# Sample states in more buffers, loads on the sync queue, and a different split of the down projection's hidden tiles

## The chip, the core and the metric

The kernel runs on one core of one Trainium2 chip. A core has TensorE (matmuls; its weight loads are listed apart as PEld), VectorE (DVE), ScalarE (ACT), GpSimd (POOL) and SyncE (SP). In this kernel SP and POOL compute almost nothing; they issue the DMA transfers, each in the order of its own instruction stream. An engine's instructions run in order, so an instruction that waits holds back everything behind it on that engine, and the same is true of a DMA issue on SP or POOL.

The metric is the device time of one execution in microseconds (us). Times are read from a profiled execution and from unprofiled repeats.

## The reference, cut to what matters

One step of a two-layer decoder on 1072 rows: 32 sample rows (8 sequences of 4), 16 meta rows and 1024 prompt rows, all of width 1024. Layer 0 mixes with two gated linear scans, layer 1 with a Mamba-2 scan. Each mixer is followed by a feed-forward network (FFN) with 2816 hidden columns, that is 22 hidden tiles of 128:

```python
def swiglu(x, w_gate, w_up, w_down):
    return (jax.nn.silu(x @ w_gate) * (x @ w_up)) @ w_down
...
    for l in range(DEPTH):
        hn = rmsnorm(x, norm_mix_pre[l])
        ...
        x = x + rmsnorm(mix.astype(x.dtype), norm_mix_post[l])
        ff = swiglu(rmsnorm(x, norm_ffn_pre[l]), ffn_w_gate[l], ffn_w_up[l], ffn_w_down[l])
        x = x + rmsnorm(ff.astype(x.dtype), norm_ffn_post[l])
```

Beside y, the step returns the new recurrent states. For the sample group a state is read, decayed, added to and written back: in layer 0 six blocks of 128 x 1024 numbers, in layer 1 32 blocks of 128 x 512.

## The kernel before

**Storage and precision.** A matrix product is made of three matmuls on split operands, high x high, low x high and high x low (`mm3`, L232 to L234). On-chip storage is 29 strips of 1072 columns, which `strip` hands out and `drop` gives back, first in, first out, beside the fixed tiles `xh` and `xl` (8 x 1072 columns each), two raw weight buffers (`raw`) and ten short-lived tiles of up to 384 columns (`tmp`, name `t`).

**Weights.** `Weights` loads raw tiles on SP (L71) into the two raw buffers, and turns them into what TensorE takes: plain units (`wh` by ACT, L129; `wl` by DVE, L130) of two strips each, or forms for a seven-product (Strassen-Winograd) 2 x 2 block scheme (sums by DVE, L97; high by ACT, L115; low by DVE, L116), a strip for four tiles, half a strip for fewer. A raw buffer is free when its last form is made. `pump(RING)` runs after each form that TensorE has used and makes forms until `RING` = 6 are ahead, or strips run out.

**An FFN, stage by stage.** (1) The first `PLAIN` = 3 hidden tiles of gate and up are plain products. (2) `quad_gu` makes hidden tiles 3 to 21, one call each: seven forms of 24 matmuls of 268 columns (the 1072 rows in four quarters of `Q` = 268; two time halves `tb`). DVE and ACT take the sums out of six PSUM banks (L419, L464, L473, L478); the next forms accumulate in the same banks, so a late DVE holds TensorE back. Hidden tiles are paired, and `store` splits seven combinations of a pair into high and low (L248 on ACT, L249 on DVE) and writes them to DRAM on POOL (L408, L409). The last hidden tile, 21, has no partner and is `alone`: `spill` splits it and writes it on SP (L633, L634). (3) `quad_down` multiplies the pairs by the down weights in five blocks of `DOWN` = (2, 2, 2, 2, 1) pairs: four output pairs p x seven forms x 2 x n x 3 matmuls of 268 columns, each form taken out of PSUM by DVE or ACT (L501, L503). The pieces of a block are fetched back from DRAM while the block before runs: some go into `xh` and `xl`, the others into strips `fo`. After each p of the last block, three adds (L514) put in the part that the halves share. (4) `kblock` multiplies the plain tiles, four of them (0, 1, 2 and 21), by their down weights: 3 column blocks b of 304, 384 and 384 columns, 8 output tiles, added to the result by DVE (L534). After each b, `side` queues the norm of that b (`postnorm` L301 to L315 and, in layer 0, the next `prenorm` L288 to L299). The next layer's first products need them (`D.need(("xn", b))`). In layer 1 the order of the b is 1, 2, 0.

**Side work.** `Driver` steps a queue of generators beside the main one: `RATE` steps for each step (one form) of the main work. During `quad_gu` of layer 0 it runs `even_samples` (rate 0.3): one strip `st`, loaded on SP (L1057), updated by DVE, written back on SP (L1073); the next load waits for that. During `quad_gu` of layer 1 it runs `odd_samples` (rate 0.55): one strip `ssm` with two states of 512 columns; `load` (L1542, on POOL) fetches state i + 1 into the buffer that state i - 1 has just been written from (L1560, on POOL). The write waits for DVE (L1558, L1559), and the load for the write to land. Both share POOL's order with the pairs' stores.

**Order.** The program's order is not quite the order on an engine: matmuls of one stage can stand among those of the stage before where their operands are ready.

Of the kernel before, what the change touches and what calls it, by code (L numbers as in the profile page):

```python
# [8 lines left out]
F32 = mybir.dt.float32  # L9
F32R = mybir.dt.float32r  # L10
# [7 lines left out]
KD = 8  # L18
# [10 lines left out]
Q = 268  # L29
# [133 lines left out]
class Core:  # L163
# [247 lines left out]
    def quad_gu(self, W, i, hook=None):  # L411


        nc = self.nc
# [5 lines left out]
        pair, odd = divmod(i - PLAIN, 2)  # L420
        alone = i == 21

# [5 lines left out]
        def second(ps, tb):  # L428

            if alone:  # L430
                self.spill(PLAIN, (2 * tb + 1) * Q, Q, gated(self.tmp(Q), ps, part(keep, 2, tb), tb))
            elif not odd:
                gated(part(hraw, 0, tb), ps, part(keep, 2, tb), tb)
            else:
                b22 = gated(self.tmp(Q), ps, part(keep, 2, tb), tb)
                t1 = part(hraw, 2, tb)
                t3 = self.tmp(Q)
                add(t3, b22, part(hraw, 0, tb), ALU.subtract)
                add(t1, b22, t1, ALU.subtract)
                self.store(pair, "s4", tb, b22)  # L440
                self.store(pair, "s3", tb, t3)
                self.store(pair, "s2", tb, t1)

        def first(ps, tb):
            hd = gated(self.tmp(Q), ps, part(keep, 0, tb), tb)
            if alone:
                self.spill(PLAIN, 2 * tb * Q, Q, hd)
            elif not odd:
                t1 = part(hraw, 2, tb)
                add(t1, part(hraw, 0, tb), hd, ALU.subtract)  # L450
                self.store(pair, "a11", tb, hd)
                self.store(pair, "s1", tb, t1)
            else:
                t4 = self.tmp(Q)
                add(t4, hd, part(hraw, 2, tb), ALU.subtract)
                self.store(pair, "a12", tb, hd)
                self.store(pair, "a22", tb, t4)
# [57 lines left out]

    def kblock(self, units, rows, acc, b, first):

        nc = self.nc
        c0, n = BLKS[b]
        for m0 in range(0, KD, KBW):  # L520
            ms = range(m0, m0 + KBW)
            pss = [self.ps(n) for m in ms]
            for i, (hi, lo) in enumerate(units):
                for m, ps in zip(ms, pss):
                    s = slice(m * P, (m + 1) * P)
                    self.mm3(ps, (hi.t[:, s], lo.t[:, s]),
                             (self.xh[:, rows[i], c0:c0 + n], self.xl[:, rows[i], c0:c0 + n]),
                             i == 0, i == len(units) - 1)
            for m, ps in zip(ms, pss):
                a = acc[m].t[:, c0:c0 + n]  # L530
                if first:
                    nc.scalar.activation(out=a, in_=ps, func=AF.Copy)
                else:
                    nc.vector.tensor_tensor(out=a, in0=a, in1=ps, op=ALU.add)  # L534
                yield

    def ffn(self, W, side, order=(0, 1, 2)):
# [25 lines left out]
        end = len(DOWN) - 1  # L563
        rows = range(1 - end % 2, KD, 2)
        pieces = lambda c: [(f, j) for f in range(7) for j in range(DOWN[c])]

# [12 lines left out]
        def fetch_plain(i):  # L579
            for dst, src in ((self.xh, self.oh), (self.xl, self.ol)):  # L580
                nc.sync.dma_start(out=dst[:, rows[i]].bitcast(F32), in_=src[:, i])

# [22 lines left out]
        for c, n in enumerate(DOWN):  # L605
            todo = [(fetch, c + 1, *x) for x in pieces(c + 1)] if c < end else [(fetch_plain, i) for i in range(PLAIN + 1)]
# [10 lines left out]
            self.drop(*own[c])  # L617
        self.drop(self.sums, *ap1)
        dn = W.take(PLAIN + 1)
        for k, b in enumerate(order):  # L620
            yield from self.kblock(dn, rows, acc, b, False)
            side(b, acc)
            if k == 0:
                W.pump(2)
        for u in dn:
            self.drop(*u)
        W.pump(4)


    def spill(self, kt, c0, n, src):  # L630
        hi, lo = self.tmp(n, F32R), self.tmp(n, F32R)
        self.split(src, hi, lo)
        self.nc.sync.dma_start(out=self.oh[:, kt, c0:c0 + n], in_=hi.bitcast(F32))  # L633
        self.nc.sync.dma_start(out=self.ol[:, kt, c0:c0 + n], in_=lo.bitcast(F32))  # L634

# [408 lines left out]
    def even_samples(self, prs):  # L1044

        nc, I, O = self.nc, self.I, self.O
        vm = self.strip(F32R, "vm")
        st = self.strip(F32, "st")
        for pr in prs:
            st_in, st_out = ("gl_in", "gl_s") if pr.gla else ("hg_in", "hg_s")  # L1050
            ks, vs = self.kst(pr)
            for e in range(2):
# [3 lines left out]
                if e == 0 or not pr.gla:  # L1056
                    nc.sync.dma_start(out=st.t[:, :1024], in_=I[st_in][:, f])  # L1057
                nc.vector.tensor_tensor(out=vm.t[:96, :1024].rearrange("p (s d) -> p s d", s=8),
                                        in0=vs[:96, e * P:(e + 1) * P].bitcast(F32).unsqueeze(1).to_broadcast([96, 8, P]),
                                        in1=self.onehot.unsqueeze(2).to_broadcast([96, 8, P]), op=ALU.mult)  # L1060
                yield
                for half in range(2):
                    ba = self.ps(512)
# [8 lines left out]
                if e == 1 or not pr.gla:  # L1072
                    nc.sync.dma_start(out=O[st_out][:, f], in_=st.t[:, :1024])  # L1073
                yield
        self.drop(vm, st, *self.kvs)

# [453 lines left out]
    def odd_samples(self, grs):  # L1530

        nc, I, O = self.nc, self.I, self.O
        sp = self.strip(F32, "ssm")
        v8 = lambda a: a.rearrange("p (h d) -> p h d", h=8)
        steps = [(gr, s) for gr in grs for s in range(8)]
        state = lambda i: sp.t[:, (i % 2) * 512:(i % 2) * 512 + 512]
        masked = lambda i: self.bxs[2].t[:, 512 + (i % 4) * P:512 + (i % 4) * P + P]
        bu = [None] * len(steps)

        def load(i):  # L1540
            gr, s = steps[i]
            nc.gpsimd.dma_start(out=state(i), in_=I["ss_in"][:, s, 512 * gr.g:512 * gr.g + 512])  # L1542
            nc.vector.tensor_scalar(out=masked(i)[:96], in0=self.bst(gr.g)[0][:96].bitcast(F32),
                                    scalar1=self.onehot[:, s:s + 1], scalar2=None, op0=ALU.mult)
# [4 lines left out]

        load(0)  # L1550
        yield
        for i, (gr, s) in enumerate(steps):
            S0 = state(i)
            if i + 1 < len(steps):
                load(i + 1)
            product(i)
# [4 lines left out]
            yield  # L1561
        self.drop(sp, *self.bxs)

# [130 lines left out]
    def ffn_units(self, l):  # L1694
# [8 lines left out]
        return s + [d[i] for i in (*range(PLAIN), 21)]  # L1703

# [4 lines left out]
PLAIN = 3  # L1709
DOWN = (2, 2, 2, 2, 1)  # L1710
RING = 6
ODD0 = 6
# [213 lines left out]
```

## Time and profile before

| | us |
|---|---|
| median of 3 runs | 3037.62 |
| lowest, highest | 3033.34, 3039.83 |
| profiled execution, its own time | 3033.33 |
| span of the profiled execution | 3031.6 |
| `quad_gu` of layer 0, by first and last matmuls | 673.3 to 1095.2 |
| `quad_down` of layer 0, four blocks of two pairs | 1095.2 to 1262.7 |
| its block of one pair, then `kblock`, taken together | 1262.7 to 1340.2 |
| first products of layer 1 after it | 1340.2 to 1437.9 |
| `quad_gu` of layer 1 | 2296.2 to 2759.2 |
| `quad_down` of layer 1, four blocks of two pairs | 2759.2 to 2926.0 |
| its block of one pair, `kblock`, last norms | 2926.0 to 3031.6 |

Positions are us from the start of the span. TensorE is busy for 95% of the span, by pipelined matmuls whose durations overlap. So its idle time by stage, and the number of matmuls that a stage gets through in a us, say more than the busy share.

### The profile page before, as it was taken

The page shows a single profiled execution, that of the slowest core. Times are in us where ns is not written, and L with a number is a line of the kernel's source. Part 1 is how long each engine was busy: PE and PEld are TensorE (multiplying, and loading weights), DVE is VectorE, ACT ScalarE, POOL GpSimd, SP SyncE. Part 2 cuts the span into 40 slices and gives each one's busy share as a digit, 9 for nine tenths or more (in the row PEclk, how much of TensorE's full clock was granted, in tenths as well). Part 3 has the DMA queues.
Part 4 walks back from the last instruction along what each step waited for, and adds up shares of the span by engine and source line. Part 5 has one row for each costly group of instructions (what it writes and reads, how often), then busy time and mean ns, then how long its engine had stood idle before and what let it go on. Part 6 is the DMA issues. An engine that isn't in the chain of part 4 may idle for free.

```text
span 3031.6 us, 54611 instructions
## 1 busy us (share of the span) xinstructions
PE 2881.8 (95%) x20386; PEld 2754.1 (91%) x20386; DVE 2242.1 (74%) x4977; ACT 1407.2 (46%) x3195; POOL 318.2 (10%) x615
## 2 busy tenths in 40 slices
PE   7999999999999999988999999999999998899996
PEld 7998989999999999988898988989999998889986
DVE  7645645687878868888877777764588787776887
ACT  6533435553434442246667585744354333335223
POOL 0000000002333310000000000000002343431000
PEclk9999999999999999999999999999999999999998
DMA  4121226334554486442444344476333554549644
GB/s 142 43 63 39 79 69 205 98 100 136 163 160 133 154 324 225 154 148 78 120 122 138 110 138 131 130 229 214 106 131 128 171 169 152 168 136 335 233 140 129
DMA packets 242169, 442.78 MB, mean 146 GB/s; under 512 B 36176, under 2 KB 172272, under 8 KB 241904
## 3 DMA queue, kind: packets, MB, share of 16 engines
q1 hardware_dynamic: 212592, 353.33, 36.6%
q0 software_dynamic: 29312, 85.97, 8.4%
q8 instruction: 160, 2.62, 0.4%
q14 instruction: 105, 0.86, 0.1%
HBM read 295.12 MB, written 144.07 MB: 145 GB/s over the span
## 4 chain that ended last, share of the span: by engine, by line
PE 41%; issue 14%; DVE 8%; POOL 6%; DMA 5%; ACT 2%; POOLq 0%; SPq 0%; DVEq 0%; ACTq 0%
PE ps L232 8%; PE ps L233 8%; PE ps L234 8%; POOL fd L409 3%; POOL fd L408 3%; PE qb L233 2%; PE qb L232 2%; PE qb L234 2%; DMA cumb<-cum_d 2%; PE qa L232 1%; PE qe L232 1%; PE qe L234 1%; PE qe L233 1%; PE qa L233 1%; PE qa L234 1%
## 5 line engine op out<-in xcount | busy, mean ns | idle before, releaser
L232 PE MATMUL ps<-xh,wh 128*128 128x384 f32 (+1 forms) x2520 | 839.3, 334 | 19.3 <-ACT xh L248 7.3
L233 PE MATMUL ps<-xh,wl 128*128 128x384 f32 (+1 forms) x2520 | 829.0, 329 | 8.8 <-DVE wl L130 8.8
L234 PE MATMUL ps<-xl,wh 128*128 128x384 f32 (+1 forms) x2520 | 829.2, 330 | 0.0
L232 PEld LDWEIGHTS ps<-xh,wh 128*128 128x128 f32 x2520 | 477.5, 190 | 43.0 <-issue 12.4
L233 PEld LDWEIGHTS ps<-xh,wl 128*128 128x128 f32 x2520 | 478.1, 190 | 15.4 <-DVE wl L130 10.8
L234 PEld LDWEIGHTS ps<-xl,wh 128*128 128x128 f32 x2520 | 476.9, 189 | 4.3 <-issue 1.9
L115 ACT ACTIVATE w_s<-sums 128x512 fp32r<-128x512 f32 (+2 forms) x292 | 147.3, 514 | 278.7 <-DVE sums L97 216.1
L232 PE MATMUL qa<-xh,w_a 128*128 128x268 f32 x688 | 201.7, 293 | 15.3 <-ACT t L478 15.2
L248 ACT ACTIVATE t<-t 128x268 fp32r<-128x268 f32 (+2 forms) x230 | 101.3, 442 | 226.7 <-DVE t L419 122.6
L408 POOL DMA_DIRECT2D fd<-t x252 | 137.0, 543 | 647.5 <-ACT t L248 619.6
L130 DVE TENSOR_TENSOR wl<-raw,wh 128x1024 fp32r<-128x1024 f32 (+1 forms) x113 | 138.1, 1224 | 85.3 <-ACT wh L129 70.8
L233 PE MATMUL qa<-xh,w_a 128*128 128x268 f32 x688 | 199.5, 290 | 0.0
L234 PE MATMUL qa<-xl,w_a 128*128 128x268 f32 x672 | 194.3, 289 | 0.0
L232 PE MATMUL qb<-t,w_s 128*128 128x268 f32 x608 | 176.2, 290 | 15.0 <-DVE t L419 14.8
L115 ACT ACTIVATE w_a<-raw 128x512 fp32r<-128x512 f32 (+2 forms) x214 | 107.3, 516 | 154.4 <-PE qb L234 52.5
L233 PE MATMUL qb<-t,w_s 128*128 128x268 f32 x608 | 174.9, 288 | 0.0
L234 PE MATMUL qb<-t,w_s 128*128 128x268 f32 x608 | 174.7, 287 | 0.0
L129 ACT ACTIVATE wh<-raw 128x1024 fp32r<-128x1024 f32 (+1 forms) x113 | 119.5, 1057 | 109.6 <-DMA raw<-in_wd 29.0
L116 DVE TENSOR_TENSOR w_s<-sums,w_s 128x512 fp32r<-128x512 f32 (+2 forms) x292 | 157.4, 546 | 16.7 <-ACT w_s L115 11.3
L232 PEld LDWEIGHTS qa<-xh,w_a 128*128 128x128 f32 x688 | 132.4, 192 | 20.1 <-ACT t L478 19.2
L116 DVE TENSOR_TENSOR w_a<-raw,w_a 128x512 fp32r<-128x512 f32 (+2 forms) x214 | 116.6, 550 | 38.1 <-ACT w_a L115 27.3
L409 POOL DMA_DIRECT2D fd<-t x252 | 137.0, 543 | 25.2 <-DVE t L249 4.8
(401 smaller groups left out, 7425.4 us busy)
## 6 DMA issues: line engine op xcount, KB each, us to landing
fd<-t POOLq DMA_DIRECT2D x504, 134.0 KB, 3.7
fo<-fd SPq DMA_DIRECT2D x54, 536.0 KB, 4.9
raw<-in_wg SPq DMA_DIRECT2D x44, 512.0 KB, 4.3
raw<-in_wu SPq DMA_DIRECT2D x44, 512.0 KB, 5.2
xh<-fd SPq DMA_DIRECT2D x40, 536.0 KB, 6.6
raw<-in_wd SPq DMA_DIRECT2D x40, 512.0 KB, 4.4
xl<-fd SPq DMA_DIRECT2D x32, 536.0 KB, 7.5
cumb<-cum_d SPq DMA_DIRECT2D x32, 512.0 KB, 5.7
```

The lines of the kernel that those rows point to most:

```text
L115: nc.scalar.activation(out=tiled(hi), in_=src, func=AF.Copy)
L116: nc.vector.tensor_tensor(out=tiled(lo), in0=src, in1=tiled(hi).bitcast(F32), op=ALU.subtract)
L129: c.nc.scalar.activation(out=hi.t[:, :w], in_=r, func=AF.Copy)
L130: c.nc.vector.tensor_tensor(out=lo.t[:, :w], in0=r, in1=hi.t[:, :w].bitcast(F32), op=ALU.subtract)
L232: nc.tensor.matmul(out, lhsT=wh, rhs=xh, start=first, stop=False, **kw)
L233: nc.tensor.matmul(out, lhsT=wl, rhs=xh, start=False, stop=False, **kw)
L234: nc.tensor.matmul(out, lhsT=wh, rhs=xl, start=False, stop=last, **kw)
L248: self.nc.scalar.activation(out=hi, in_=src, func=AF.Copy)
L408: self.nc.gpsimd.dma_start(out=self.fd[:, i, FORMS.index(f), o:o + Q], in_=hi.bitcast(F32))
L409: self.nc.gpsimd.dma_start(out=self.fd[:, i, FORMS.index(f), 2 * Q + o:2 * Q + o + Q], in_=lo.bitcast(F32))
```

## The change

The diff does four things.

- `odd_samples` gets two strips, that is four states; `load` is issued on SP and three steps ahead; the mask that it used to make (L1543) becomes a step of its own, still one ahead. `even_samples` gets two strips `st`; the load of the next state is issued on SP one state ahead, and the write moves from SP to POOL.
- `RING` falls from 6 to 5.
- `DOWN` becomes (2, 2, 2, 2). `ALONE` = 19: hidden tiles 19, 20 and 21 have no partner, and `REST` lists the six plain tiles of the down projection: 0, 1, 2, 19, 20, 21. So `kblock` multiplies six tiles instead of four. The operands of the last two lie in four `fo` strips, the others in `xh` and `xl`.
- The `alone` tiles are written by `spill` on POOL instead of SP.

```diff
-        alone = i == 21
+        alone = i >= ALONE
...
-                self.spill(PLAIN, 2 * tb * Q, Q, hd)
+                self.spill(REST.index(i), 2 * tb * Q, Q, hd, nc.gpsimd)
...
         def fetch_plain(i):
-            for dst, src in ((self.xh, self.oh), (self.xl, self.ol)):
-                nc.sync.dma_start(out=dst[:, rows[i]].bitcast(F32), in_=src[:, i])
+            if i < 4:
+                plain.append([x[:, 2 * i + 1 - end % 2] for x in (self.xh, self.xl)])
+            else:
+                own[-1] += [self.strip(F32R, "fo") for _ in range(2)]
+                plain.append([x.t for x in own[-1][-2:]])
+            for dst, src in zip(plain[i], (self.oh, self.ol)):
+                nc.sync.dma_start(out=dst.bitcast(F32), in_=src[:, i])
...
-        dn = W.take(PLAIN + 1)
+        dn = W.take(len(REST))
...
     def even_samples(self, prs):
-        st = self.strip(F32, "st")
+        states = [self.strip(F32, "st") for _ in range(2)]
...
-                    nc.sync.dma_start(out=st.t[:, :1024], in_=I[st_in][:, f])
+                    done += 1
+                    st = states[done % 2]
...
+                if e == 0 or not pr.gla:
+                    load(done + 1)
...
-                    nc.sync.dma_start(out=O[st_out][:, f], in_=st.t[:, :1024])
+                    nc.gpsimd.dma_start(out=O[st_out][:, f], in_=st.t[:, :1024])
...
     def odd_samples(self, grs):
-        sp = self.strip(F32, "ssm")
+        sp = [self.strip(F32, "ssm") for _ in range(2)]
...
-        state = lambda i: sp.t[:, (i % 2) * 512:(i % 2) * 512 + 512]
+        state = lambda i: sp[i // 2 % 2].t[:, (i % 2) * 512:(i % 2) * 512 + 512]
...
-            nc.gpsimd.dma_start(out=state(i), in_=I["ss_in"][:, s, 512 * gr.g:512 * gr.g + 512])
+            nc.sync.dma_start(out=state(i), in_=I["ss_in"][:, s, 512 * gr.g:512 * gr.g + 512])
+
+        def mask(i):
+            gr, s = steps[i]
...
-        load(0)
+        for i in range(3):
+            load(i)
+        mask(0)
         yield
         for i, (gr, s) in enumerate(steps):
             S0 = state(i)
+            if i + 3 < len(steps):
+                load(i + 3)
             if i + 1 < len(steps):
-                load(i + 1)
+                mask(i + 1)
             product(i)
...
-DOWN = (2, 2, 2, 2, 1)
-RING = 6
+DOWN = (2, 2, 2, 2)
+ALONE = PLAIN + 2 * sum(DOWN)
+REST = (*range(PLAIN), *range(ALONE, 22))
+RING = 5
```

More of the change, by code (lines that the diff above doesn't have):

```diff
@@ L430, in second @@
             if alone:
-                self.spill(PLAIN, (2 * tb + 1) * Q, Q, gated(self.tmp(Q), ps, part(keep, 2, tb), tb))
+                self.spill(REST.index(i), (2 * tb + 1) * Q, Q, gated(self.tmp(Q), ps, part(keep, 2, tb), tb), nc.gpsimd)
             elif not odd:
@@ L514, in quad_down, with kblock @@
                 nc.vector.tensor_tensor(out=a, in0=a, in1=x, op=ALU.add)
-    def kblock(self, units, rows, acc, b, first):
+    def kblock(self, units, right, acc, b, first):
         nc = self.nc
@@ L526, in kblock @@
                     self.mm3(ps, (hi.t[:, s], lo.t[:, s]),
-                             (self.xh[:, rows[i], c0:c0 + n], self.xl[:, rows[i], c0:c0 + n]),
+                             [x[:, c0:c0 + n] for x in right[i]],
                              i == 0, i == len(units) - 1)
@@ L563, in ffn @@
         end = len(DOWN) - 1
-        rows = range(1 - end % 2, KD, 2)
+        plain = []
         pieces = lambda c: [(f, j) for f in range(7) for j in range(DOWN[c])]
@@ L605, in ffn @@
         for c, n in enumerate(DOWN):
-            todo = [(fetch, c + 1, *x) for x in pieces(c + 1)] if c < end else [(fetch_plain, i) for i in range(PLAIN + 1)]
+            todo = [(fetch, c + 1, *x) for x in pieces(c + 1)] if c < end else [(fetch_plain, i) for i in range(len(REST))]
             every, count = 4 * 7 // len(todo), [0]
@@ L616, in ffn @@
                 yield from self.quad_down(W, right(c), n, p, acc, ap1, c, paced)
-            self.drop(*own[c])
-        self.drop(self.sums, *ap1)
-        dn = W.take(PLAIN + 1)
+            if c < end:
+                self.drop(*own[c])
+        last = own[end]
+        self.drop(self.sums, *ap1, *last[:-4])
+        dn = W.take(len(REST))
         for k, b in enumerate(order):
-            yield from self.kblock(dn, rows, acc, b, False)
+            yield from self.kblock(dn, plain, acc, b, False)
             side(b, acc)
@@ L626, in ffn, with spill @@
             self.drop(*u)
+        self.drop(*last[-4:])
         W.pump(4)
-    def spill(self, kt, c0, n, src):
+    def spill(self, kt, c0, n, src, queue=None):
+        queue = queue or self.nc.sync
         hi, lo = self.tmp(n, F32R), self.tmp(n, F32R)
         self.split(src, hi, lo)
-        self.nc.sync.dma_start(out=self.oh[:, kt, c0:c0 + n], in_=hi.bitcast(F32))
-        self.nc.sync.dma_start(out=self.ol[:, kt, c0:c0 + n], in_=lo.bitcast(F32))
+        queue.dma_start(out=self.oh[:, kt, c0:c0 + n], in_=hi.bitcast(F32))
+        queue.dma_start(out=self.ol[:, kt, c0:c0 + n], in_=lo.bitcast(F32))
     def fetch(self, k0, b):
@@ L1047, in even_samples, with load @@
         vm = self.strip(F32R, "vm")
-        st = self.strip(F32, "st")
+        states = [self.strip(F32, "st") for _ in range(2)]
+        loads = [(name, i) for name, n in (("hg_in", 4), ("gl_in", 2)) for i in range(n)]
+        done = -1
+        def load(i):
+            if i < len(loads):
+                nc.sync.dma_start(out=states[i % 2].t[:, :1024], in_=I[loads[i][0]][:, loads[i][1]])
+        load(0)
         for pr in prs:
@@ L1056, in even_samples @@
                 if e == 0 or not pr.gla:
-                    nc.sync.dma_start(out=st.t[:, :1024], in_=I[st_in][:, f])
+                    done += 1
+                    assert loads[done] == (st_in, f)
+                    st = states[done % 2]
                 nc.vector.tensor_tensor(out=vm.t[:96, :1024].rearrange("p (s d) -> p s d", s=8),
@@ L1072, in even_samples @@
                 if e == 1 or not pr.gla:
-                    nc.sync.dma_start(out=O[st_out][:, f], in_=st.t[:, :1024])
+                    nc.gpsimd.dma_start(out=O[st_out][:, f], in_=st.t[:, :1024])
                 yield
-        self.drop(vm, st, *self.kvs)
+        self.drop(vm, *states, *self.kvs)
     def kslot(self):
@@ L1561, in odd_samples @@
             yield
-        self.drop(sp, *self.bxs)
+        self.drop(*sp, *self.bxs)
     def sgate(self, gr):
@@ L1702, in ffn_units @@
             t += 2 * n
-        return s + [d[i] for i in (*range(PLAIN), 21)]
+        return s + [d[i] for i in REST]
 OP = 1
```

## The prediction

> **What bounds the kernel now.** The page first: TensorE's busy share and the line of its granted clock.
>
> ```profile
> span 3031.6 us, 54611 instructions
> ...
> PE 2881.8 (95%) x20386; PEld 2754.1 (91%) x20386; DVE 2242.1 (74%) x4977; ACT 1407.2 (46%) x3195; POOL 318.2 (10%) x615
> ...
> PEclk9999999999999999999999999999999999999998
> ```
>
> TensorE is the bound on the whole, so a gain can only come from its idle time, from a low clock, or from fewer matmul columns. The second view, busy time by stretch, shows where these are. Columns: stretch, its length, then for each engine busy us (instructions), granted clock, DMA share, GB/s.
>
> ```profile
> 673.30:1095.20 421.90, 405.03 (x3211) 400.93 (x3210) 340.26 (x722) 171.80 (x387) 136.98 (x252) 0.99 0.51 162
> 2296.20:2759.20 463.00, 421.84 (x3225) 411.41 (x3226) 357.56 (x788) 172.16 (x390) 171.88 (x316) 0.97 0.52 170
> 2759.20:2926.00 166.80, 166.80 (x1350) 166.70 (x1350) 130.99 (x369) 54.86 (x157) 0.00 (x0) 1.00 0.70 241
> 1262.70:1300.00 37.30, 32.09 (x220) 29.96 (x219) 34.84 (x90) 6.93 (x14) 0.32 (x1) 0.95 0.39 126
> 1300.00:1340.20 40.20, 39.28 (x233) 38.57 (x232) 34.42 (x75) 18.41 (x32) 0.00 (x0) 1.00 0.51 154
> 1340.20:1437.90 97.70, 80.97 (x454) 76.74 (x453) 81.45 (x164) 58.83 (x110) 0.77 (x7) 0.91 0.29 93
> 3004.00:3031.60 27.60, 3.33 (x14) 2.20 (x14) 20.85 (x46) 6.38 (x12) 0.00 (x0) 0.62 0.45 148
> 1170.00:1220.00 50.00, 50.00 (x407) 50.00 (x407) 42.83 (x117) 12.27 (x34) 0.00 (x0) 1.00 0.70 239
> ```
>
> The last row gives the price of a matmul of 268 columns when nothing holds it: 50.00 / 407 = 0.123 us. By columns, one of 304 is 0.139 and one of 384 is 0.176. The 19 x 168 = 3192 matmuls of a `quad_gu` stage then need 392 us. Layer 0 (first row) takes 421.9, with 16.9 idle; layer 1 (second row), the same matmuls, 463.0, with 41.2 idle. The four blocks of two pairs (third row) have no idle at all. The block of one pair (fourth row) has DVE busy for 34.8 of 37.3 us: there DVE is the bound. After `kblock` (sixth row) TensorE idles 16.7 us at a clock of 0.91.
>
> Next, who holds TensorE in the two `quad_gu` stages. The waits view of TensorE alone, layer 1 (first three rows, all there are) and layer 0 (last two). Columns: us, times, longest.
>
> ```profile
> PE qb L232 <- DVE t L419: 33.1, 22, 3.6
> PE qa L232 <- ACT t L478: 6.0, 8, 1.2
> PE qe L232 <- DVE keep L419: 1.9, 2, 1.6
> ...
> PE qa L232 <- ACT t L478: 9.3, 8, 1.8
> PE qb L232 <- DVE t L419: 7.6, 7, 1.8
> ```
>
> Never a weight form; always DVE or ACT late at emptying a bank. Why they are late, from the same view for all engines, layer 1:
>
> ```profile
> POOL ssm L1542 <- DMA out_ss_s<-ssm: 58.1, 22, 5.4
> DVE ssm L1558 <- DMA ssm<-in_ss_in: 50.4, 27, 4.2
> POOL out_ss_s L1560 <- DVE ssm L1559: 46.0, 8, 10.0
> ACT w_a L115 <- DMA raw<-in_wg: 18.7, 9, 3.0
> DVE sums L97 <- DMA raw<-in_wu: 17.7, 11, 3.2
> ACT t L248 <- DMA fd<-t: 14.3, 10, 2.5
> ```
>
> POOL stands 58.1 us for a state's write to land before it may issue the load into that buffer. DVE then stands 50.4 us for the load, with the emptying of the banks queued behind; and the pairs' stores queue behind POOL's wait, so that the ten `tmp` tiles come free late (the last row). Layer 0 has neither wait.
>
> **The change, part by part.** *Odd states, four buffers, on SP.* Load i + 3 still waits for write i - 1, but state i + 3 is used three steps later. A step is 2 / 0.55 = 3.6 forms of 24 x 0.123 = 2.95 us, about 10.7 us; three of them far exceed the longest wait, 5.4, plus the landing, 3.5:
>
> ```profile
> ssm<-in_ss_in POOLq DMA_DIRECT2D x32, 256.0 KB, 3.5
> L1542 POOL DMA_DIRECT2D ssm<-in_ss_in x32 | 17.7, 554 | 428.4 <-PE qe L234 369.4 <-DMA out_ss_s<-ssm 58.1
> L408 POOL DMA_DIRECT2D fd<-t x252 | 137.0, 543 | 647.5 <-ACT t L248 619.6
> L1548 PE MATMUL ps<-bxs 96*128 96x512 f32 x32 | 13.2, 411 | 0.0
> L1064 PE MATMUL ps<-vm,kvs 96*128 96x512 f32 x16 | 6.4, 397 | 0.0
> ```
>
> So both waits go, and POOL also loses 32 issues of 0.554, 17.7 us, which are off the path. What is late next? The raw weights, and DVE's own work: the two waits for `raw` above, and a DVE that is busy 357.6 us. At layer 0's length that would be 85% where layer 0 has 81%. I therefore set layer 1's stage at layer 0's 421.9, plus 13.2 - 6.4 = 7 for the additional state products, plus a new cost. The load now stands on SP, where the raw weights (L71) queue behind it until write i - 1 has landed. No row shows that wait on SP. From below it costs nothing (a raw load has to wait for its own buffer anyway); from above, 22 waits of 2.6, or 58 us, all handed on. I take 6, near the lower end, since four forms of lead (below) stand between a raw load and TensorE, and the DVE stall is what remains. 422 + 7 + 6 = 435: **-28**, bounds 0 and -50 (the idle 41.2 and 9.8, what is left of the 16.8 of additional busy time after 7; the clock is 0.97).
>
> *Even states, two buffers; `RING` 5; alone tiles on POOL.* Strips: 16 for the transformed inputs, 3 for `keep`, `sums`, `hraw`, 5 for the states, so 5 of 29 are left: one form in use and four ahead, 11.8 us instead of 14.7. A form needs a raw load of some 4.3 (page, `raw<-in_wg`, below) and about 1.3 of ACT and DVE; and no row shows TensorE waiting for a form in these stages. I cost it at 0; if that cover goes, the price is in the rivals. A state's write on SP used to hold raw loads until DVE was done; on POOL, pairs' stores queue behind it, which come from later DVE work anyway. The six POOL writes come in place of others: pairs' stores fall by 28 issues, the spills on POOL are 24, at 0.543 each, all off the path. One pair less means 6 splits and 8 combinations less on DVE, 14 x 0.43 = 6 us in each layer. Layer 0's stage: **-4**, bounds +8 (a raw wait as large as the one removed) and -16.9, its idle.
>
> ```profile
> raw<-in_wg SPq DMA_DIRECT2D x44, 512.0 KB, 4.3
> L503 DVE TENSOR_TENSOR acc<-acc,qb x208: 423/428/435, 1102.0 to 2960.0; 128x268 f32<-128x268 f32 x104
> L130 DVE TENSOR_TENSOR wl<-raw,wh 128x1024 fp32r<-128x1024 f32 (+1 forms) x113 | 138.1, 1224 | 85.3 <-ACT wh L129 70.8
> 1307.48 0.85 DVE L534 TENSOR_TENSOR acc<-acc,ps 128x304 f32<-128x304 f32 x2
> 1343.73 0.86 DVE L249 TENSOR_TENSOR xl<-t,xh 128x304 fp32r<-128x304 f32 x2
> 1381.90 1.03 DVE L249 TENSOR_TENSOR xl<-t,xh 128x384 fp32r<-128x384 f32 x2 [0.95 <-ACT xh L248]
> 1417.91 0.55 DVE L249 TENSOR_TENSOR xl<-t,xh 128x384 fp32r<-128x384 f32 x1
> 2993.33 1.95 DVE L534 TENSOR_TENSOR acc<-acc,ps 128x384 f32<-128x384 f32 x4
> 3013.24 0.47 DVE L534 TENSOR_TENSOR acc<-acc,ps 128x304 f32<-128x304 f32 x1
> ```
>
> *The block of one pair becomes two plain tiles.* TensorE loses 168 x 0.123 = 20.7 and gains 2 x (24 x 0.139 + 48 x 0.176) = 23.6: +2.9 per layer. DVE loses 56 additions of 0.428, 24 us, and the forms' work, and gains two `wl` of 1.224; the three adds at L514 move into the fourth block, where DVE (131.0 of 166.8) has room. What counts is when the norms can start. From the timeline above, layer 0: the last additions of the first b of `kblock` end at 1308.3, 45.6 after the block of one pair began (1262.7). The norms of the three b are then ready at 1344.6, 1382.9 and 1418.5: 38 us and 36 us apart, a chain longer than the products beside it (six units of 24 matmuls, 20 to 25 us), so TensorE idles for it.
>
> After the change `kblock` starts at 1262.7 on that scale, and its first b is 144 x 0.139 = 20 us. It can't be that fast at once: six units need six raw loads through two buffers and twelve conversions. I add 9 us (two raw loads of 4.3) and 1.5 for the additions, so the first norm starts near 1293 instead of 1308: 15 us sooner. The chain keeps its length, and its end moves with it: **-15**. Bounds: 0 (the conversions hold it) and -30 (16.7 of idle, 8.8 of clock, 5.2 of idle in the fourth row). With six tiles there are fewer spare strips, so only two of the next layer's units can be made before `kblock` ends, where there were about five. Their wait is hidden by the chain of norms; uncovered it would be three conversions of 1.2 and a load, 8 us, inside the bound.
>
> At the end of layer 1 the chain has only the last norms. The last addition now comes at 3013.2, though only 14 matmuls are left after 3004 (seventh row): DVE is still at the second norm, which it began behind the additions at 2993.3. 18.4 us follow. After, from 2926: lag 5, b 1 and 2 of 25.3 each and b 0 of 20.2 end at 3002, with the second norm done by then (it starts at 2982 and takes 3013 - 2993 = 20). Then 18.4: 3020.6 instead of 3031.6. With a lag of 7, **-9**, bounds 0 and -13.
>
> **Sum:** -28 - 4 - 15 - 9 = -56. The profiled execution took 3033.3 (span 3031.6 and 1.7 around it), 4.3 below the median of the runs. So 3033.3 - 56 + 4.3 = 2981.6; I say 2981.
>
> **Rivals.** *The queue makes no difference* (0.20): the wait for the write to land is the same pair of transfers, moved from POOL to SP, where raw weights stand behind it and DVE waits for them at L97 instead of at L1558. For it: L97 and L115 already wait 36.4 us for raw weights in layer 1. Against it: three steps of lead, and layer 0, which has loads of states on SP and loses only 16.9. It takes away the -28: 3009. The Trainium skill, "DMA: Bandwidth & Descriptors", section "Issuing engines are not separate DMA queues", speaks for it: all queues feed the same engines, so another issuing queue saves only issue time. By that rule, too, layer 1 would keep its 463.0 us.
>
> *All idle of these stages goes* (0.08): -50, -17, -25 and -12, 2934. Against it: layer 0's idle has no state wait in it.
>
> *Slower: too short a lead* (0.08). A hidden tile's first forms need raw weights whose buffers come free only when the two last forms of the tile before are made. If the lost form of lead reaches TensorE, each of 38 hidden tiles stops for 2.95 us, 112 in all, and the result is 3037.6 - 56 + 112 = 3094. It decides from 56 / 38 = 1.5 us per hidden tile. Against it: no wait for a form in either stage now.
>
> *It does not amount to much* (0.04): that stall at about 1.5, or a gain only where bounds meet: within 0.2% of 3037.6.
>
> **How the numbers follow.** Forecast 0.60 at 2981, the two rivals on the gain's size 0.20 at 3009 and 0.08 at 2934, nothing 0.04, slower 0.08. Differences below 0.2%, 6 us, can't be told from none in a measurement of this kernel. So faster 0.88, same 0.04, slower 0.08. The range leaves out 2934, nothing and slower, 0.20 together, and reaches past 3009 by 7 for the other terms: 2948 to 3016.
>
> **What would show it.** Right: no wait of POOL for `out_ss_s` and none of DVE L1558 for a load; layer 1's `quad_gu` stage near 435 us, layer 0's near 418; last additions of the first b of `kblock` near 30 us after the fourth block of two pairs, norms still 36 to 38 apart. Wrong: TensorE waiting for `w_a` or `w_s` (too short a lead); SP's waits for `out_ss_s` in the tens of us with L97's waits for raw risen by as much (the queue); a `kblock` that waits for `wl` by more than 9 us, or norms further apart.

## The result, and the profile after

The changed kernel takes 2984.93 us, the median of four runs (2980.86 to 2995.97), beside 3038.72 for the kernel before, also of four runs: a ratio of 0.9832, with a 95% interval of 0.9801 to 0.9862. A second measurement, told below, gives 0.985 (0.9821 to 0.988). The forecast was 2981 us, with a range of 2948 to 3016.

First the busy time by stretch in the kernel after: layer 0's `quad_gu`, the boundary from the end of the down projection to the last norm, layer 1's `quad_gu`, and the end. Columns as in the prediction: stretch, length, busy us of TensorE, weight loads, DVE, ACT and POOL with their instructions, granted clock, DMA share, GB/s.

```profile
672.20:1088.50 416.30, 404.98 (x3211) 401.37 (x3210) 334.95 (x707) 169.90 (x380) 135.30 (x250) 0.99 0.51 162
1254.30:1397.70 143.40, 132.38 (x786) 128.36 (x785) 102.70 (x212) 66.30 (x130) 0.82 (x7) 0.95 0.33 102
2281.30:2718.60 437.30, 411.34 (x3223) 404.60 (x3224) 350.02 (x774) 168.55 (x384) 149.37 (x276) 0.99 0.55 178
2884.70:2980.10 95.40, 75.99 (x460) 74.33 (x458) 56.24 (x113) 23.07 (x39) 0.00 (x0) 0.90 0.32 103
```

The same view of the kernel before, for the two stretches of which the prediction shows only parts:

```profile
1262.70:1418.50 155.80, 132.94 (x793) 125.88 (x792) 131.43 (x289) 70.31 (x141) 0.93 (x7) 0.93 0.36 114
2925.50:3031.60 106.10, 75.53 (x462) 70.88 (x461) 84.62 (x191) 27.14 (x50) 0.00 (x0) 0.89 0.38 122
```

Layer 1's `quad_gu` falls from 463.0 to 437.3 us, layer 0's from 421.9 to 416.3. The boundary row begins 3 us ahead of the first product of `kblock` (1257.4); counted from there, the last norm is ready after 140.3 us instead of 155.8. The last row, too, begins a little early, and counted from the first product of the last `kblock` (2887.2) the end takes 92.9 instead of 106.1.

Where do the 25.7 us of layer 1 come from? The waits view of the kernel after, in that stage (us in total, times, longest); the last line is of SP's queue, over the whole run.

```profile
PE qb L232 <- DVE t L419: 20.6, 13, 3.2
ACT w_a L115 <- DMA raw<-in_wg: 64.7, 15, 6.4
DVE sums L97 <- DMA raw<-in_wu: 16.1, 14, 2.9
DVE ssm L1586 <- DMA ssm<-in_ss_in: 16.8, 18, 2.8
SPq L1563 <- DMA out_ss_s<-ssm: 244.3, 28, 15.0
```

TensorE's wait for DVE is down from 33.1 to 20.6 us. POOL no longer waits for a write to land. But DVE still waits for loads of states, 16.8 us in 18 waits (50.4 in 27 before), although every load is issued three states ahead. SP now holds 244.3 us for writes to land; ACT's wait for raw weights has risen from 18.7 to 64.7 us, DVE's (L97) has not (17.7 and 16.1). No wait of TensorE for a weight form appears. The wait for a load is the riddle that the experiments take up first.

The DVE timeline at the boundary, kernel after (start, us, operation, and in brackets the idle time before it and what ended it):

```profile
1276.50 1.71 DVE L534 TENSOR_TENSOR acc<-acc,ps 128x304 f32<-128x304 f32 x4 [4.72 <-PE ps L234]
...
1288.73 2.13 DVE L534 TENSOR_TENSOR acc<-acc,ps 128x384 f32<-128x384 f32 x4 [8.40 <-PE ps L234]
1293.26 0.47 DVE L263 SCALAR_TENSOR_TENSOR t<-b_kt,t 128x304 f32<-128x304 f32 x1 [2.40 <-ACT t L262]
...
1317.96 0.47 DVE L249 TENSOR_TENSOR xl<-t,xh 128x304 fp32r<-128x304 f32 x1
...
1358.29 1.02 DVE L249 TENSOR_TENSOR xl<-t,xh 128x384 fp32r<-128x384 f32 x2
...
1397.16 0.55 DVE L249 TENSOR_TENSOR xl<-t,xh 128x384 fp32r<-128x384 f32 x1
```

The last additions of the first b end at 1278.2, 20.8 us after `kblock` began, and not 30 us as forecast. The norms are then ready at 1318.4, 1359.3 and 1397.7: 40, 41 and 38 us one after the other, 119.5 in all from 1278.2, where the kernel before had 110.2. The second row shows why to suspect `kblock` itself: DVE stands idle for 8.4 us for products of the *next* b, and only then goes on with the norm of the first one (L263).

### The profile page after: what moved, and what is told of

Same layout as the page of the kernel before. It is cut to its first block, busy times and chain, and to the rows that moved or that the text cites. A ratio compares the mean times of both kernels' runs of the same rounds, so it can differ in the third digit from the quotient of the medians.

```text
span 2980.1 us, 54172 instructions
## 1 busy us (share of the span) xinstructions
PE 2871.4 (96%) x20338; PEld 2753.4 (92%) x20338; DVE 2171.9 (73%) x4753; ACT 1388.3 (47%) x3131; POOL 298.2 (10%) x581
## 4 chain that ended last, share of the span: by engine, by line
PE 33%; issue 23%; DVE 8%; DMA 6%; POOL 4%; ACT 2%; POOLq 0%; DVEq 0%; SPq 0%; ACTq 0%
PE ps L232 5%; PE ps L233 5%; PE ps L234 5%; PE qb L232 2%; PE qb L233 2%; PE qb L234 2%; POOL fd L409 2%; POOL fd L408 2%; PE qa L232 2%; PE qe L232 2%; PE qe L234 1%; PE qe L233 1%; PE qa L233 1%; PE qa L234 1%; DMA raw<-in_wd 1%
## 5 line engine op out<-in xcount | busy, mean ns | idle before, releaser
L115 ACT ACTIVATE w_s<-sums 128x512 fp32r<-128x512 f32 (+1 forms) x264 | 138.8, 535 | 159.5 <-DVE sums L97 88.3
L115 ACT ACTIVATE w_a<-raw 128x512 fp32r<-128x512 f32 (+1 forms) x194 | 101.8, 538 | 236.8 <-DMA raw<-in_wg 119.1
L232 PE MATMUL qa<-xh,w_a 128*128 128x268 f32 x672 | 193.3, 288 | 3.9 <-ACT t L478 3.6
L233 PE MATMUL qa<-xh,w_a 128*128 128x268 f32 x672 | 192.4, 286 | 0.0
L408 POOL DMA_DIRECT2D fd<-t x224 | 121.3, 541 | 600.1 <-ACT t L248 584.9
L116 DVE TENSOR_TENSOR w_a<-raw,w_a 128x512 fp32r<-128x512 f32 (+1 forms) x194 | 111.7, 579 | 77.6 <-ACT w_a L115 66.7
L116 DVE TENSOR_TENSOR w_s<-sums,w_s 128x512 fp32r<-128x512 f32 (+1 forms) x264 | 150.1, 574 | 24.1 <-ACT w_s L115 12.0
L232 PEld LDWEIGHTS qa<-xh,w_a 128*128 128x128 f32 x672 | 126.5, 188 | 6.7 <-ACT t L478 5.5
L233 PEld LDWEIGHTS qa<-xh,w_a 128*128 128x128 f32 x672 | 126.6, 188 | 0.6
```

What stands on the lines that cost most here:

```text
L115: nc.scalar.activation(out=tiled(hi), in_=src, func=AF.Copy)
L116: nc.vector.tensor_tensor(out=tiled(lo), in0=src, in1=tiled(hi).bitcast(F32), op=ALU.subtract)
L232: nc.tensor.matmul(out, lhsT=wh, rhs=xh, start=first, stop=False, **kw)
L233: nc.tensor.matmul(out, lhsT=wl, rhs=xh, start=False, stop=False, **kw)
L408: self.nc.gpsimd.dma_start(out=self.fd[:, i, FORMS.index(f), o:o + Q], in_=hi.bitcast(F32))
```

## The experiments

Each run has the kernel before beside it on the same chip, and the ratios below are to that; times in us from different rows can come from different chips. The stages are cut in the same way in every profile: `quad_gu` of layer 1 from its first product into `qa` to the first addition of the down projection (L503), which makes it 5 to 8 us longer than in the rows above; the boundary from the first L503 of layer 0 to the last norm (L249); the end from the first L503 of layer 1. Boundary and end so take in the whole down projection, and are longer than in the rows above. The stages of the kernel before come from one profile, taken on the chip of the first result.

| kernel | ratio (95%) | `quad_gu`, layer 1 | DVE waits for state loads there | boundary | end |
|---|---|---|---|---|---|
| before | | 468.3 | 50.4 | 317.9 | 267.1 |
| after | 0.9832 (0.9801 to 0.9862) | 445.6 | 16.8 | 301.3 | 253.2 |
| after, again | 0.985 (0.9821 to 0.988) | 443.9 | 14.9 | 300.0 | 253.1 |
| states alone | 0.995 (0.9934 to 0.9965) | 453.0 | 18.2 | 316.1 | 265.2 |
| split alone | 0.9895 (0.9871 to 0.9918) | 460.8 | 46.1 | 301.2 | 252.2 |
| `RING` 5 alone | 1.0013 (1.0002 to 1.0024) | 471.8 | 50.9 | 322.8 | 266.6 |
| after, loads on POOL | 0.9887 (0.987 to 0.9904) | 458.5 | 39.9 | 299.7 | 253.6 |
| after, decay in turn | 0.9819 (0.9792 to 0.9845) | 433.0 | none | 300.7 | 252.4 |
| the same, loads on POOL | 0.9816 (0.979 to 0.9843) | 432.7 | 2.3 | 299.0 | 252.1 |
| split alone, decay in turn | 0.9784 (0.9762 to 0.9806) | 431.5 | 1.3 | 301.0 | 252.7 |
| before, decay in turn | 0.9905 (0.9881 to 0.9929) | 439.1 | 1.7 | 323.9 | 265.2 |
| after, norm banks | 0.9787 (0.9759 to 0.9814) | 447.6 | 14.5 | 288.8 | 248.3 |
| after, both | 0.9734 (0.9711 to 0.9756) | 435.3 | none | 289.5 | 246.8 |
| after, both, loads on POOL | 0.9719 (0.9701 to 0.9736) | 433.5 | 2.3 | 289.0 | 247.5 |

A stage in one profiled execution is uncertain by some us: the first 673 us, which no edit touches, take 669.4 to 679.4 in these profiles.

### The parts of the change, one at a time

*States alone:* the changed kernel with the old split.

```diff
-DOWN = (2, 2, 2, 2)
+DOWN = (2, 2, 2, 2, 1)
```

> Four and two state buffers, loads on SP, writes on POOL and RING 5, but the old split of the down projection (five blocks of pairs, four plain tiles; only tile 21 alone, written on POOL). Theory (the state buffers carry the gain of the quad_gu stages, the split that of the ends): layer 1's quad_gu stage near 437 us (463 before), layer 0's near 418 (422 before), the last norm of layer 0 and the end of layer 1 as before (155.8 and 106.1 us): about -31 us, a ratio near 0.990. Rival (one pair less on DVE is what relieves quad_gu): layer 1's stage at 450 or more, ratio 0.994 or higher.

*Split alone:* the changed kernel with the two sample functions of before and the old ring.

```diff
-        sp = [self.strip(F32, "ssm") for _ in range(2)]
+        sp = self.strip(F32, "ssm")
...
-            nc.sync.dma_start(out=state(i), in_=I["ss_in"][:, s, 512 * gr.g:512 * gr.g + 512])
+            nc.gpsimd.dma_start(out=state(i), in_=I["ss_in"][:, s, 512 * gr.g:512 * gr.g + 512])
...
-RING = 5
+RING = 6
```

> Only the new split (four blocks of two pairs, six plain tiles, alone tiles written on POOL); one strip of states in each layer on the old queues, RING 6. Theory: the boundary after layer 0's FFN 12 to 16 us shorter, the end 11 to 13 shorter, layer 1's quad_gu stage at 455 to 463 with POOL's wait for out_ss_s still near 58 us: -24 to -30 us, ratio near 0.991. Rival (one pair less on DVE relieves quad_gu): layer 1's stage at 450 or less, ratio 0.988 or less. If both this and the states alone are as the theory says, the two gains add up to the whole -51 or so.

The states alone give half of what the theory asked, 0.995 instead of 0.990 (15 us of 3030): layer 1's stage falls by 15 us, not by 26. The split alone gives 0.9895 (32 us); its boundary and end are those of the whole change, and layer 1's stage falls by 7.5 too, with POOL's wait for writes still at 59.3 us. By its numbers the rival of the first run is met (450 us or more, 0.994 or higher), while the second run is near its theory. So neither is right alone: the two gains add up to 1.55% (1.5 to 1.7% measured for the change), and a third of layer 1's gain belongs to the split. The split takes a pair with its splits and combinations off DVE, whose busy time in this stage falls from 359.2 to 355.9 us; that this is what brings the 7.5 us is argued and not shown.

*`RING` 5 alone,* in the kernel before.

```diff
-RING = 6
+RING = 5
```

> The kernel before with RING 5 alone. Theory: no wait of TensorE for a form in either quad_gu stage, both stages within 3 us of before, ratio 0.998 to 1.002. Rival (the lead was needed): TensorE waits for w_a or w_s, each quad_gu stage 10 us longer or more, ratio 1.007 or higher.

The theory holds nearly: no wait of TensorE for a form, and a ratio of 1.0013, whose interval (1.0002 to 1.0024) stands for a loss of 1 to 7 us and not for the rival's. Layer 1's stage is 3.5 us longer in this one profile, where the theory allowed 3.

### Queue or buffers: the loads on POOL again

```diff
-            nc.sync.dma_start(out=state(i), in_=I["ss_in"][:, s, 512 * gr.g:512 * gr.g + 512])
+            nc.gpsimd.dma_start(out=state(i), in_=I["ss_in"][:, s, 512 * gr.g:512 * gr.g + 512])
```

> The changed kernel with the loads of the odd states on POOL again (four buffers, three states ahead); nothing else. Theory (the buffers matter, not the queue): DVE L1586 hardly waits for a load, SP no longer waits for out_ss_s and ACT L115 waits for raw again nearer to the 18.7 us of before than to 64.7; POOL waits for out_ss_s again, tens of us, and the pairs' stores stand behind that; layer 1's quad_gu stage 433 to 443, total within 6 us of the changed kernel, ratio to before 0.981 to 0.986. Rival (the queue matters): the stage back at 455 or more, ratio 0.989 or higher.

The stage goes back to 458.5 us and the ratio to 0.9887. By the stage the rival wins (455 us or more; the ratio is just short of its 0.989): with four buffers on POOL, layer 1 gains only 2 us on the split alone (460.8). But *why* would DVE mind the queue if the load came three states early? The waits of this kernel in that stage:

```profile
POOL ssm L1563 <- DMA out_ss_s<-ssm: 56.2, 18, 5.9
DVE ssm L1586 <- DMA ssm<-in_ss_in: 39.9, 24, 5.7
```

DVE waits for the loads nearly as it did with two buffers. That can't be if a state lies loaded for three steps before it is touched. One view answers it, the instructions of the tile `ssm` (count, min/median/max ns, first and last start), here of the changed kernel:

```profile
L1563 SPq DMA_DIRECT2D ssm<-in_ss_in x32: 327/328/426, 2285.6 to 2626.9; - x32
L1586 DVE TENSOR_TENSOR ssm<-ssm,cd x32: 682/692/694, 2288.4 to 2630.3; 128x512 f32<-128x512 f32 x32
L1587 DVE TENSOR_TENSOR ssm<-ssm,ps x32: 677/680/687, 2289.4 to 2673.3; 128x512 f32<-128x512 f32 x32
```

The last load starts at 2626.9, the last decay (L1586) at 2630.3, and the last addition (L1587) only at 2673.3, 43 us or some three to four states later. On DVE the order is, nearly throughout, decay of state i + 3, addition of state i. The likely reason, argued from the program alone: the decay needs nothing but the load, so when the program was put in order for DVE it was placed as soon as the load could be there, three states ahead of its own addition. The three steps of lead lie between the decay and the addition, where they are of no use; between the load and its first reader there is no lead at all. In the kernel before the same view shows the two 12.5 us apart, which is one state:

```profile
L1558 DVE TENSOR_TENSOR ssm<-ssm,cd x32: 681/693/694, 2307.5 to 2695.9; 128x512 f32<-128x512 f32 x32
L1559 DVE TENSOR_TENSOR ssm<-ssm,ps x32: 675/680/689, 2313.8 to 2708.4; 128x512 f32<-128x512 f32 x32
```

### The decay in its turn

The decay of state i is ordered behind the addition of state i - 1. Both are on DVE, so this adds no wait for a semaphore and no work; it only fixes the order.

```diff
-            nc.vector.tensor_tensor(out=v8(S0), in0=v8(S0), in1=gr.cd[:, :, s:s + 1].to_broadcast([P, 8, 64]), op=ALU.mult)
-            nc.vector.tensor_tensor(out=S0, in0=S0, in1=bu[i], op=ALU.add)
+            decay = nc.vector.tensor_tensor(out=v8(S0), in0=v8(S0), in1=gr.cd[:, :, s:s + 1].to_broadcast([P, 8, 64]), op=ALU.mult); i and self.behind(decay, self.added)
+            self.added = nc.vector.tensor_tensor(out=S0, in0=S0, in1=bu[i], op=ALU.add)
...
+def behind(self, x, y):
+    self.tc.add_manual_dep(x.ins, y.ins.name, mybir.DependencyInfo(
+        mybir.DependencyClass.NoSync, mybir.DependencyReason.DATA), reason="behind")
```

Four kernels have this edit and no other beside it: the changed kernel with the loads on SP and with the loads on POOL, the split alone (two buffers, POOL), and the kernel before with nothing else. The changed kernel itself was measured beside the first two.

> The changed kernel once more, on the chip of the next three, so that they can be set beside it and not only beside the kernel before: a ratio of 0.980 to 0.986 if the first result holds here too; near 0.988, that of the loads on POOL, if that difference was one between chips and not between queues.

> The changed kernel, with the decay of odd state i (L1586) held on DVE behind the addition of state i - 1 (L1587). In the changed kernel DVE's order has the decay three states ahead of the addition, so that it asks for a load as soon as that is issued. Theory (this eats the lead, and DVE's waits for loads are handed on to TensorE): DVE's 16.8 us of waiting for loads fall below 4, layer 1's quad_gu stage from 445.6 us (first product to first addition of the down projection) to 434 to 441, ratio to before 0.002 to 0.004 below the changed kernel's. Rival (DVE's own work and SP's waits set the stage): the waits go, the stage stays within 3 us, the same ratio.

> The loads of the odd states on POOL, with the decay in turn as in the run before. Theory (POOL was worse only because a load on POOL comes later and the decay asks for it at once): DVE's 39.9 us of waiting for loads fall below 5, the stage falls from 458.5 us to 440 to 448 and the ratio to 0.982 to 0.985, though POOL still waits 50 us or more for writes to land. Rival (POOL's own waits do the harm, through the pairs' stores behind them): the stage stays at 453 or more, ratio 0.987 or higher.

The changed kernel repeats at 0.985. With the decay in turn, the instructions of `ssm` (loads on SP):

```profile
L1563 SPq DMA_DIRECT2D ssm<-in_ss_in x32: 327/328/426, 2279.8 to 2612.6; - x32
L1586 DVE TENSOR_TENSOR ssm<-ssm,cd x32: 677/682/693, 2282.4 to 2639.6; 128x512 f32<-128x512 f32 x32
L1587 DVE TENSOR_TENSOR ssm<-ssm,ps x32: 673/676/689, 2283.4 to 2654.6; 128x512 f32<-128x512 f32 x32
```

The last decay now stands 15 us ahead of the last addition instead of 43, the last load 27 us ahead of that decay instead of 3.4, DVE's list of waits has no load of a state left, and the stage is 433.0 us instead of 443.9. By stretch, the changed kernel again and the one with the decay in turn:

```profile
2286.80:2730.70 443.90, 420.49 (x3280) 414.28 (x3281) 353.80 (x783) 173.01 (x395) 151.55 (x280) 0.98 0.56 182
```

```profile
2275.50:2708.50 433.00, 416.26 (x3280) 410.98 (x3281) 351.86 (x782) 172.67 (x395) 151.55 (x280) 0.99 0.57 187
```

The same 3280 products and the same DVE work in 11 us less. The runs' medians are 2981.23 and 2971.51, a gain of the same size; the two ratios' intervals overlap, so it is the stage and the waits that carry this reading. On POOL the edit brings 26 us, from 458.5 to 432.7, and the two queues are now alike (0.9816 and 0.9819), though POOL still waits 68.2 us for writes to land and SP holds 249.9. So the theory holds in both runs, by stages somewhat shorter than it asked for (434 and 440 us at the least), and the queue by itself costs or gains nothing that these runs can tell. It counted only while the decay asked for each load at once: there a load on SP came sooner than one behind POOL's stores and waits, which is argued from DVE's 16.8 against 39.9 us.

> The split alone (one strip of states in each layer, loads on POOL, RING 6), with the decay of odd state i behind the addition of state i - 1. Theory (two buffers still suffer: a load can't be issued before the write of the state before last has landed, and POOL's order delays it): DVE's waits for loads fall from 46.1 us to 10 to 30, layer 1's quad_gu stage from 460.8 to 446 to 456, ratio 0.985 to 0.988. Rival (the order on DVE was all of it, the buffers nothing): the waits below 5, the stage at 430 to 438, ratio 0.980 to 0.982, as with four buffers in turn.

> The kernel before with one thing changed: the decay of odd state i (L1558) behind the addition of state i - 1 (L1559). Two buffers, loads on POOL, RING 6 and the old split stay. Theory (the order on DVE was what held layer 1's quad_gu stage; the state buffers of the change only eased it): DVE's 50.4 us of waiting for loads fall below 5, the stage (first product to first addition of the down projection) from 468.3 to 436 to 446, boundary and end as before, ratio 0.988 to 0.992, below the 0.995 of the state buffers alone. Rival (the order helps only beside the new split): the stage at 450 or more, ratio 0.994 or higher.

With two buffers the rival wins: 431.5 us, as good as with four, and a ratio of 0.9784. With the decay in turn, then, the state part of the change adds nothing that can be seen. The waits in that stage:

```profile
POOL ssm L1551 <- DMA out_ss_s<-ssm: 67.3, 23, 5.6
DVE ssm L1567 <- DMA ssm<-in_ss_in: 1.3, 1, 1.3
PE qb L232 <- DVE t L419: 10.7, 8, 1.9
ACT w_a L115 <- DMA raw<-in_wg: 22.5, 13, 3.0
```

POOL waits for the writes as ever (58.1 before), yet DVE hardly waits for a load, and TensorE's wait for DVE is 10.7 us, where the split alone had 28.2. In the kernel before, the edit alone gives 439.1 us and 0.9905 (25 us of 3030), as its theory had it, and more than all of the state part of the change (0.995). The end stays as it was; the boundary is 6 us longer in this profile, no more than the untouched first stretch varies. Its row by stretch beside that of the kernel before, cut alike:

```profile
2296.20:2764.50 468.30, 427.14 (x3268) 416.71 (x3269) 359.24 (x793) 174.84 (x397) 171.88 (x316) 0.97 0.53 173
```

```profile
2299.00:2738.10 439.10, 419.42 (x3268) 413.22 (x3269) 358.22 (x792) 175.87 (x397) 171.88 (x316) 0.98 0.57 185
```

The stage takes 29 us less, by the order of 32 instructions on one engine. The additional buffers, the longer lead and the other queue had eased this wait and not removed it. The split's own share stays beside it: 439.1 to 431.5 us with the decay in turn, 468.3 to 460.8 without.

### The norm's banks

The norm's mean is a product into one of two PSUM banks, `kt` or `sc`. `kblock` takes its banks in turn from all eight, those two among them; and it lets the norm step on only after a group of four output tiles. So the mean of the first b can have to wait until DVE has emptied products of the next b out of its bank, and these come only after six units. The edit keeps `kblock` to the other six banks and steps the norm between units.

```diff
-        dn = W.take(len(REST))
+        dn = W.take(len(REST)); self.pstags = ["mm0", "mm1", "mm2", "a0", "a1", "o"]
...
-        self.drop(*last[-4:])
+        self.drop(*last[-4:]); self.pstags = None
...
                              i == 0, i == len(units) - 1)
+                if i < len(units) - 1: yield
```

> The changed kernel, with kblock's products kept out of the two PSUM banks that the norm's mean uses (six banks in turn instead of eight) and the norm stepped between the units of a group, so that the mean needn't wait for the additions of the next b. Theory (this made the chain of norms longer, 119.6 us instead of 110.2): DVE's 8.4 us of idle before L534 goes, the first two norms stand 34 to 37 us after one another, the last norm of layer 0 is ready 6 to 12 us sooner after the down projection's start, the end a few us: ratio 0.002 to 0.004 below the changed kernel's. Rival (the chain is bound by its own operations, DVE 102.7 of 143.4 us): no change. Second rival (six banks are too few): TensorE waits for L534 and kblock gets longer, ratio 0.001 or more above.

The gain is there, and larger than expected: 2960.95 us beside the 2981.23 of the changed kernel on the same chip. In the profiles, 16 of the 20 us lie in the boundary and the end; 5 are in the first stretch, which the edit doesn't touch. From the DVE timeline of this kernel:

```profile
1274.83 1.71 DVE L534 TENSOR_TENSOR acc<-acc,ps 128x304 f32<-128x304 f32 x4 [4.54 <-PE ps L234]
1276.46 2.20 DVE L284 TENSOR_TENSOR t<-t 128x304 f32<-128x304 f32 x4
1282.31 0.47 DVE L263 SCALAR_TENSOR_TENSOR t<-b_kt,t 128x304 f32<-128x304 f32 x1 [3.65 <-ACT t L262]
```

L263 follows the end of the last additions (1276.5) by 5.8 us, where it took 15.1 in the changed kernel (1278.2 to 1293.3), and no L534 stands between. In the kernel before it took 9.8 (1308.3 to 1318.1), with such a group of additions between:

```profile
1313.63 2.10 DVE L534 TENSOR_TENSOR acc<-acc,ps 128x384 f32<-128x384 f32 x4
1318.13 0.47 DVE L263 SCALAR_TENSOR_TENSOR t<-b_kt,t 128x304 f32<-128x304 f32 x1 [1.26 <-ACT t L262]
```

The product of the mean itself, in the changed kernel:

```profile
1290.99 0.71 PE L256 MATMUL b_kt<-t,ones 128*128 128x304 f32 x2
```

It starts 0.1 us after the four additions of the next b have ended (1288.73 + 2.13), and as much after them in the kernel before (at 1315.84). So for the first norm the trace shows the wait for the bank. The chains by stretch, from the last additions of the first b to the last norm: the kernel before, after, and with this edit.

```profile
1308.30:1418.50 110.20, 92.55 (x518) 87.61 (x517) 88.98 (x184) 58.49 (x119) 0.61 (x6) 0.92 0.33 105
```

```profile
1278.20:1397.70 119.50, 108.48 (x613) 104.46 (x612) 88.36 (x188) 57.28 (x118) 0.82 (x7) 0.94 0.30 92
```

```profile
1276.50:1383.90 107.40, 105.47 (x619) 103.03 (x618) 87.95 (x188) 57.63 (x118) 0.82 (x7) 1.00 0.32 102
```

DVE has 88 us of work in each; the chain in the changed kernel was longer by waiting alone. With the edit TensorE is busy for 105.5 of 107.4 us, and the granted clock goes to 1.00. It is the first norm that comes 10 us sooner (30.2 instead of 40.2 after the additions); the others follow by 41.6 and 35.5. The theory's 34 to 37 us between the first two were not met, and what holds the second norm is not shown. Six banks are enough: TensorE shows no wait for L534. The two halves of the edit weren't tried apart.

### Both together

> The changed kernel with both edits: decay in turn, loads on SP, and the norm's two banks kept free with the norm stepped between units. The two act in different stages, so they should add up: layer 1's quad_gu stage at 432 to 437, last norm of layer 0 near 289 us after the down projection's start, ratio 0.985 - 0.003 - 0.006 = 0.976, 0.973 to 0.979. Rival (a gain at the boundary is lost again in the following stage): 0.979 or higher.

> As the run with both edits, with the odd states' loads on POOL. Theory (with the lead real, the queue makes no difference: SP's 245 us of holding and POOL's 68 us of waiting both cost nothing): within 0.002 of the run with the loads on SP, the quad_gu stage within 3 us. Rival (SP's holding costs): 0.002 to 0.004 below it; (POOL's waiting costs): as much above.

They add up, and a little more: 0.9734 with the loads on SP, 0.9719 with the loads on POOL (2947.61 us), within 0.002 of one another, and the stages are those of the single edits. This last kernel is the fastest of all, 1.1 to 1.3% below the change. The boundary's gain isn't lost later.

## Why the prediction was right, and where it was not

The time, 2985 for 2981, came out right, and that is in part luck: several of its steps failed, with errors that cancelled.

- **Odd states, -28.** The stage's length was right: 437.3 us for the 435 forecast. The step that failed is "state i + 3 is used three steps later", and with it "so both waits go". POOL's wait went; DVE's stayed at 16.8 us, because DVE's order touches a state as soon as it is loaded. The states by themselves brought 15 us. The sum came out because a term was missing on the other side: one pair less on DVE, worked out as 6 us in each layer, was counted for layer 0 alone, and in layer 1 the split brought 7.5. The lead could have been had by ordering the decay, which alone brought 29 us in the kernel before.
- **SP holds raw weights, +6.** SP does hold, 244.3 us. But with the decay in turn, loads on SP and on POOL give the same stage: the holding costs nothing that can be measured. Of the sign that was named for the queue only the first half came, since L97's waits for raw weights did not rise (17.7 before, 16.1 after). ACT's longer wait for raw weights (64.7 us) isn't SP's holding either, as it is 68.8 with the loads on POOL; ACT has room for it. It is 61.3 with the states alone, 22.9 with `RING` 5 alone and 19.4 with the split alone, so it came with the additional states. Whether by the strip that they take, alone or together with `RING` 5, no run shows.
- **`RING` 5 at 0.** A loss of 1 to 7 us by the interval of its run, which is near nothing. The slower rival, a lead that is too short, didn't occur: no wait of TensorE for a form.
- **Even states, -4.** Layer 0's stage is 416.3 us for 418. In the profiles of all kernels here, cut at the first addition, it spreads from 419.9 to 428.0, so in a single profile a gain of this size can't be told from none. Taken together, the eight profiles of kernels with the whole change have a mean of 422.2 us there, the three of the kernel before, with `RING` 5 and with the decay in turn 426.4, which fits the forecast. The even states were not tried apart.
- **The boundary, -15.** Measured 15.5, out of two errors of opposite sign. "I add 9 us" for six conversions was wrong: TensorE waits for none of them, and the additions of the first b ended after 20.8 us. "The chain keeps its length" was wrong by as much: it grew from 110.2 to 119.5 us. Of these 9.3 us, 5.3 are the first norm's (L263 after 15.1 us instead of 9.8): a group of six units lasts longer, and the mean waits behind it for its bank. The rest was not traced. The edit to the norm's banks takes more away than had been added, down to 107.4.
- **The end, -9.** Measured 11 to 14, depending on where the stage is cut (10.9 together with the blocks ahead of it, 13.9 from the first addition).
- **Writes on POOL, 0.** The 28 stores that fall away are those of one layer, the 24 spills those of both; as all are off the path, the sum doesn't change.
- **What is left open.** The parts sum to more than the whole: between the last norm and layer 1's `quad_gu`, unchanged code, the changed kernel takes 883.6 us for 877.7, and so do most kernels with the split (882.9 to 885.8; two take 879.8 and 876.3), while those without it take 872.3 to 877.7. This was not settled.
- **The rivals.** "The queue makes no difference" had its premise right and its price wrong: it would have left layer 1 at 463, but the queue wasn't what held it. The rule of the Trainium skill that spoke for it, "DMA: Bandwidth & Descriptors", section "Issuing engines are not separate DMA queues", agrees with the runs with the decay in turn (433.0 and 432.7 us). The 445.6 and 458.5 us with the decay ahead differ, as argued above, by when an engine's order lets a load start, of which that rule says nothing. "All idle goes" (2934) was the nearest to what the stages hold: the two edits together come to 0.9719 of the kernel before.

## What to carry to other kernels

A lead is the distance between a load and its *first reader in the engine's own order*, not between two lines of the program; before adding buffers, compare the first and last starts of the load, its first reader and its last one. Where an engine waits for a load that should have been early, try to order that reader behind the work that it has overtaken: here this brought more than two strips, a queue and a longer lead. And when a stage is given more work per group, look at which banks or buffers a side chain shares with it, since the chain then waits for a whole group.

## What was not expected of the hardware

The granted clock goes with much of the spread between runs of the same kernel. The split alone ran in 2984.72 us at a clock of 0.991 and in 3008.2 at 0.984, so 0.7% of clock goes with 0.8% of time; the fastest kernel was granted 0.990 or 0.991 in all its runs, the changed one 0.984 or 0.985 in its second measurement. In the boundary the clock rose from 0.94 to 1.00 when the idle time of TensorE went, and 619 products were then busy for 105.5 us where 613 had been for 108.5. The chain is 12.1 us shorter, of which 9.1 were idle time of TensorE: here the gap cost 3 us more than its own length.
